# A hybrid attention block: the GLA state scan written in two halves, weights' loads in program order, first scalings without precedence

## The chip, the cores and the metric

The kernel runs on one core of a Trainium2 chip. The metric is the device time of one execution in microseconds (us); the time before is the median of three runs. Engines are named as in the profile: PE multiplies matrices, DVE and POOL work elementwise, ACT evaluates functions and copies, SP only issues DMAs. Each engine works through its own instructions in order; between engines there are semaphores.

## The reference

One encoder block over 1024 tokens of width 1024, in float32. Eight heads of neighbourhood attention (`y_na`) stand beside four heads of bidirectional gated linear attention (GLA); both are projected from the same normalised input, joined, projected out, and followed by a squared-ReLU MLP.

```python
n = rmsnorm(h, ln_g)
proj = n @ w_in                      # q, k, v of both groups, gate r, decay factors z_f, z_b
...
# GLA, per head and direction, in chunks of 64 tokens
A = jnp.where(mask, jnp.einsum('bhnid,bhnjd->bhnij', q_dec, k_inv), 0.0)
o_intra = jnp.einsum('bhnij,bhnje->bhnie', A, v)
contrib = jnp.einsum('bhncd,bhnce->bhnde', k * jnp.exp(b_last - b), v)
def step(S, inp):
    g, c = inp
    return g[..., None] * S + c, S
_, S_prev = lax.scan(step, S0, (decay, contrib))
o = o_intra + jnp.einsum('bhncd,bhnde->bhnce', q_dec, S_prev)
...
h = h + concat(y_na, y_gla) @ w_out
h = h + square(relu(rmsnorm(h) @ w1)) @ w2
```

## The kernel before

Activations lie transposed: features on the 128 partitions, tokens along the free axis, in two halves of 512. Every product of 32-bit precision is made of three matmuls of rounded parts: high by high, low by high, high by low (`product`). A projection block is 128 columns of `w_in`: for each half 8 steps of three 128x512 matmuls.

PE's matmuls are kept in the order of the program (class `Ordered`). All other instructions are ordered by a scheduler that takes what is ready, with precedence for what stands in `tc.high_priority`; a larger offset means further ahead. `tc.keep_in_program_order` takes single instructions out of this freedom. `SOON` is 200, `SOON_W` 100, `SOON_B` 300.

- Start, to about 55 us: x is loaded in four quarters of 256 tokens, scaled and split (`do_x`), and its reciprocal norm `rms` is made (`do_norm`, L220 to L230: ACT Ln, Exp and Square, DVE products). Meanwhile PE makes z (decay factors, banks z0 and z1 of the PSUM tag "mm"), and q and k of head group 0 (banks sb and ob). `z_evac` scales z (zf, L342) and splits it into zT (L343 on ACT, L344 on DVE); `qk_evac` scales q and k for two heads each (qd, kd, L280, and ACT's copies in L281). The tag "mm" has two banks, so projection 4's second half needs z1's.
- `weights` (L164 to L177) brings the weights of one projection block: wf by SP (L169), ACT writes wl = -wf (L173), POOL issues an accumulating DMA that adds the exact weights to it (L174), which leaves the low part, and ACT casts the high part wh (L176). Two buffers of each exist. The first block is split by POOL.
- GLA, heads h = 0 to 3 (`gla_contrib`, `gla_scan`, `gla_within`, `gla_intra`, `gla_inter`): contributions per chunk go to the states st; the scan (L591 forward on the lower partitions, L594 backward on the upper ones) is 28 DVE steps; `gla_within` makes masked scores of half a sequence on PE (a, two banks of tag "s") and DVE copies them under a mask into asb (L586, selF then selB). The second half's scores need the first half's banks. Between these stages PE gets steps of the projections of blocks 8, 5, 9, 1, 3, 6, 7, 11, 10, 12, 16, 20, 13, 17, 21 and so on, as many as the row of `GLA_FILL` for this head says; element i is run at `fill.at(GLA_FILL, h, i)`.
- Neighbourhood attention (about 262 to 450 us), pairs of heads p = 0 to 3: `bias_for` loads the relative bias bt from a DRAM scratch (SP, L742; 16 earlier copies fill the scratch, L443), adds the mask msk (POOL's DMA, L736) on DVE (L747); `softmax` makes scores sc, adds the bias with a running extreme (L802), takes the exponential on ACT (L804) and scales (L806, L807); `turn` transposes (pt). bt0, the first bias tile, lies in memory that head 3's kI occupied.
- Then the output projection and the MLP, which fill the span to its end.

Of the kernel before, what the change touches and what calls it, by code (L numbers as in the profile page):

```python
# [14 lines left out]
ALU = mybir.AluOpType  # L15
# [14 lines left out]
NCH = T // CH  # L30
# [14 lines left out]
)  # L45
FILL_ORDER = (('v', 0), ('r', 0), ('v', 1), ('r', 1), ('q', 1), ('v', 2), ('v', 3), ('r', 3), ('r', 2), ('n', 0), ('k', 0))

# [1 line left out]
SOON = 200  # L49
# [17 lines left out]
def block_kernel(ctx, tc, xT, g_mix, w_in, w_z, rpb, na_mask, gu, gb, g_gla, sel_f, sel_b,  # L67
                 rst, w_out, g_ff, w1, w2, g_fin, out):
    nc = tc.nc
    V, S, DMA, G = nc.vector, nc.scalar, nc.sync, nc.gpsimd  # L70
# [14 lines left out]
    def bank(tag, name):  # L85
        return ps.tile([P, H], F32, tag=tag, name=name)
# [77 lines left out]
    def weights(block, eng=None):  # L164


        with tc.high_priority(offset=SOON_W):
            wf = stg.tile([P, D], F32, tag="wf", name="wf")
            DMA.dma_start(wf, block)  # L169
            if eng is not None:  # L170
                return split(wf, eng)
            wl = stg.tile([P, D], F32R, tag="wl", name="wl")
            tc.keep_in_program_order(S.activation(wl, wf, AF.Copy, scale=-1.0))  # L173
            G.dma_start(wl, block, accum_op=ALU.add)  # L174
            wh = stg.tile([P, D], F32R, tag="wh", name="wh")
            tc.keep_in_program_order(S.copy(wh, wf))  # L176
            return wh, wl  # L177
# [12 lines left out]
    def split(wf, eng=None, steps=1):  # L190
        wh = stg.tile([P, D], F32R, tag="wh", name="wh")
        wl = stg.tile([P, D], F32R, tag="wl", name="wl")
        for i in range(steps):
            c = slice(i * D // steps, (i + 1) * D // steps)
            S.copy(wh[:, c], wf[:, c])
            (eng or V).tensor_tensor(wl[:, c], wf[:, c], wh[:, c].bitcast(F32), op=ALU.subtract)
        return wh, wl
# [70 lines left out]
    def qk_evac(g, which):  # L268

        dic, sc, t = ((qd, 0.125, "q"), (kd, 1.0, "k"))[which]  # L270
        for i in range(2):
            dic[2 * g + i] = (g0 if t == "q" and i else gk).tile([P, T], F32, tag={"k0": "k00", "q0": "k10", "k1": "k20"}.get(f"{t}{i}", "qd1"), name=f"{t}d{2*g+i}")

        def ev(hf, d):
            c = slice(hf * H, (hf + 1) * H)
            for i in range(2):
                dst = dic[2 * g + i]
                a, b = (slice(0, 64), slice(64, 128))[::1 - 2 * i]
                with tc.high_priority(offset=SOON):
                    V.scalar_tensor_tensor(dst[a, c], d[a, :], sc, rms[a, c], op0=ALU.mult, op1=ALU.mult)  # L280
                S.copy(dst[b, c], dst[a, c])  # L281
        return ev
# [152 lines left out]
    def bias_cols(cs):  # L435
        for c in cs:
            for dl in range(3):
                o = 8 * dl + 7 - c
                DMA.dma_start(rpb1[c, :, dl, :, :], rpb[:, :, o:o + CW])
# [6 lines left out]
    with pool("gla", R) as gp:  # L446
# [42 lines left out]
        def make_masks():  # L489
            selF = gp.tile([P, 1, P], F32, tag="selF", name="selF")  # L490
            selB = gp.tile([P, 1, P], F32, tag="selB", name="selB")
            G.dma_start(selF, sel_f)
            G.dma_start(selB, sel_b)
            asb = [gp.tile([P, 4, P], F32, tag=f"asb{i}", name=f"asb{i}") for i in range(2)]
            for a in asb:
                G.memset(a, 0.0)
            masks.extend([selF, selB, asb])
# [23 lines left out]
        def gla_keys(h, b):  # L521

            b3 = b.rearrange("p (n c) -> p n c", c=CH)
            kD = g0.tile([P, T], F32, tag="kD", name=f"kD{h}")
            dec = gp.tile([P, NCH], F32, tag="dec", name=f"dec{h}", bufs=2)
            bl = gp.tile([P, NCH], F32, tag="bl", name=f"bl{h}")
            for (lo, hi, e) in ((0, 64, CH - 1), (64, 128, 0)):
                V.tensor_copy(bl[lo:hi, :], b3[lo:hi, :, e])
            S.activation(dec, bl, AF.Exp, scale=-1.0 / 16)
            V.tensor_tensor(kD.rearrange("p (n c) -> p n c", c=CH), b3,  # L530
                            bl.unsqueeze(2).to_broadcast([P, NCH, CH]), op=ALU.subtract)
            S.activation(kD, kD, AF.Exp, scale=1.0 / 16)
            V.tensor_tensor(kD, kD, kd[h], op=ALU.mult)
            qD = gp.tile([P, T], F32, tag="qD", name=f"qD{h}", bufs=2)
            kI = gp.tile([P, T], F32, tag="kI", name=f"kI{h}", bufs=2)
            S.activation(kI, b, AF.Exp, scale=1.0 / 16)
            V.tensor_tensor(kI, kI, kd[h], op=ALU.mult)
            S.activation(qD, b, AF.Exp, scale=-1.0 / 16)
            V.tensor_tensor(qD, qD, qd[h], op=ALU.mult)
            return dec, kD, qD, kI  # L540

        def gla_ktok(h, kD):

            kt = g0.tile([P, NCH // 2, P], F32, tag="kt", name=f"kt{h}", bufs=2)
            for hf in range(2):
                tb = bank("t", f"kt{h}_{hf}")
                for i in range(4):
                    j = hf * 4 + i
                    PE.transpose(tb[:, i * P:(i + 1) * P], kD[:, j * P:(j + 1) * P], ident)
                S.copy(kt[:, hf * 4:(hf + 1) * 4, :], tb.rearrange("p (a b) -> p a b", a=4))  # L550

            st = gp.tile([P, NCH, P], F32, tag="st", name=f"st{h}")
            G.memset(st[0:64, 0, :], 0.0)
            G.memset(st[64:128, NCH - 1, :], 0.0)
            return kt, st
# [19 lines left out]
        def gla_within(h, hf, qD, kI):  # L575

            selF, selB, asb = masks
            a = [bank("s", f"a{h}_{hf}_{i}") for i in range(2)]
            for i in range(4):
                j = hf * 4 + i  # L580
                for dr_ in range(2):
                    o = 64 * dr_
                    PE.matmul(a[dr_][:, i * P:(i + 1) * P], kI[o:o + 64, j * P:(j + 1) * P],
                              qD[o:o + 64, j * P:(j + 1) * P], start=True, stop=True)
            for sel, src in ((selF, a[0]), (selB, a[1])):
                V.copy_predicated(asb[hf], sel.bitcast(U32).to_broadcast([P, 4, P]),  # L586
                                  src.rearrange("p (a b) -> p a b", a=4))

        def gla_scan(dec, st):
            for i in range(1, NCH - 1):  # L590
                V.scalar_tensor_tensor(st[0:64, i + 1, :], st[0:64, i, :], dec[0:64, i:i + 1],  # L591
                                       st[0:64, i + 1, :], op0=ALU.mult, op1=ALU.add)
                j = NCH - 1 - i
                V.scalar_tensor_tensor(st[64:128, j - 1, :], st[64:128, j, :], dec[64:128, j:j + 1],  # L594
                                       st[64:128, j - 1, :], op0=ALU.mult, op1=ALU.add)
# [48 lines left out]
        for h in range(GH):  # L644
            if not masks:
                make_masks()
            fill.until(("q", h // 2))
            dec, kD, qD, kI = gla_keys(h, bs[h])
            fill.at(GLA_FILL, h, 0)
            kt, st = gla_ktok(h, kD)  # L650
            bias_cols(range(2 * h, 2 * h + 2))
            fill.at(GLA_FILL, h, 1)
            fill.until(("v", h))
            gla_contrib(h, kt, st, 0)
            fill.at(GLA_FILL, h, 2)
            gla_contrib(h, kt, st, 1)
            gla_scan(dec, st)
            fill.at(GLA_FILL, h, 3)
            gla_within(h, 0, qD, kI)
            fill.at(GLA_FILL, h, 4)  # L660
            gla_within(h, 1, qD, kI)
            fill.at(GLA_FILL, h, 5)
            if h + 1 < GH:
                bs[h + 1] = gla_gates(h + 1)
            ob = [gla_intra(h, 0)]
            fill.at(GLA_FILL, h, 6)
            ob.append(gla_intra(h, 1))
            fill.at(GLA_FILL, h, 7)
            sq = [gla_inter(0, ob[0], st, qD)]
            fill.at(GLA_FILL, h, 8)  # L670
            sq.append(gla_inter(1, ob[1], st, qD))
            fill.at(GLA_FILL, h, 9)
            gla_norm(h, 0, ob[0], sq[0])
            fill.at(GLA_FILL, h, 10)
            gla_norm(h, 1, ob[1], sq[1])
# [279 lines left out]
    wf = stg.tile([P, D], F32, tag="wf", name="wf")  # L955
# [337 lines left out]
    with tc.high_priority(offset=150):  # L1293
        for n in range(2):
            p, i = f1.order[n]
# [241 lines left out]
```

## Time and profile before

| | us |
|---|---|
| runs | 1219.82, 1216.45, 1217.22 |
| median | 1217.22 |
| profiled execution | 1217.29 |
| its span, first to last instruction | 1215.5 |
| mean granted clock of PE | 0.986 |

A row of the timeline gives start and length in us, engine, line, operation, output<-inputs, shape and count; in brackets the idle time of the engine just ahead and what ended it. Rows with a count stand for several instructions merged. A row of waits gives engine, operation and line that waited, what it waited for, and then the us in total, the times and the longest. A row of windows is explained where it is used. DMA rows of the chain run from issue to landing.

### The profile page before, as it was taken

To read this page: it belongs to the slowest core of one execution; us is meant where nothing else is said; L and a number is where in the kernel's file an instruction comes from. 1 tells how busy PE (TensorE), PEld (TensorE's weight loads), DVE (VectorE), ACT (ScalarE), POOL (GpSimd) and SP (SyncE) were. 2 spreads that over 40 slices of the span, in tenths; PEclk is the share of its full clock that TensorE was granted. 3 is DMA by queue.
4 is the path that set the end of the run, shared out by engine and by line. 5 is a ranking of instruction groups with operands and counts; after the bars stand their busy time and mean duration, and the time that the engine had idled before them with its cause. 6 is when DMAs were issued, how large, how long until landed. Compare 5 with 4: busy or idle time off the path is not lost.

```text
span 1215.5 us, 15429 instructions
## 1 busy us (share of the span) xinstructions
PE 1158.5 (95%) x5632; PEld 948.7 (78%) x5632; DVE 874.8 (72%) x1558; ACT 665.1 (55%) x1222; POOL 248.3 (20%) x199
## 2 busy tenths in 40 slices
PE   8899899887999999998999999999999999999995
PEld 8778688675877878876778888888888888888775
DVE  8578768735768696675877885876858768587467
ACT  6667566643756674544643744545445454453664
POOL 5100000201120223441103140321403214032004
PEclk9999999998999999999999999999999999999998
DMA  7332231312323324230110111112111111111203
GB/s 233 70 90 56 72 70 36 89 27 80 68 50 83 70 75 164 104 138 1 58 64 18 70 65 56 37 52 70 62 57 38 53 70 57 59 42 52 70 1 139
DMA packets 40283, 84.03 MB, mean 69 GB/s; under 512 B 9264, under 2 KB 20656, under 8 KB 40208
## 3 DMA queue, kind: packets, MB, share of 16 engines
q1 hardware_dynamic: 36608, 71.11, 17.4%
q0 software_dynamic: 3456, 11.94, 5.5%
q8 instruction: 44, 0.72, 0.2%
q14 instruction: 31, 0.25, 0.1%
q10 hardware_dynamic: 144, 0.00, 0.0%
HBM read 78.85 MB, written 5.96 MB: 70 GB/s over the span
## 4 chain that ended last, share of the span: by engine, by line
PE 71%; DVE 15%; ACT 8%; issue 3%; DMA 2%; SPq 0%; POOL 0%; DVEq 0%; ACTq 0%
PE f L114 24%; PE u L114 21%; PE proj L114 13%; PE op L114 5%; PE sc L114 2%; PE o L114 2%; PE no L114 2%; DVE st L594 1%; PE pt L119 1%; DVE st L591 1%; DVE nl L309 1%; DMA bt<-rpb 1%; DVE pl L1010 1%; DVE asb L586 1%; DVE nf L940 1%
## 5 line engine op out<-in xcount | busy, mean ns | idle before, releaser
L1032 ACT CAST ph<-A 128x512 fp32r<-128x512 f32 x166 | 103.0, 621 | 146.5 <-PE f L114 73.6
L1010 POOL TENSOR_TENSOR ul<-uB,uh 128x512 fp32r<-128x512 f32 x84 | 109.1, 1317 | 330.5 <-ACT uh L1045 213.4
L114 PE MATMUL f<-uh,ph 128*128 128x512 f32 x400 | 155.8, 390 | 1.5 <-ACT u L1053 1.4
L114 PE MATMUL proj<-nh,wh 128*128 128x512 f32 x352 | 151.4, 430 | 4.7 <-DVE zf L342 4.7
L114 PE MATMUL f<-ul,ph 128*128 128x512 f32 x400 | 155.8, 389 | 0.1
L114 PE MATMUL f<-uh,pl 128*128 128x512 f32 x400 | 155.7, 389 | 0.0
L1010 DVE TENSOR_TENSOR pl<-A,ph 128x512 fp32r<-128x512 f32 x166 | 112.8, 689 | 52.5 <-ACT ph L1032 52.5
L114 PE MATMUL proj<-nh,wl 128*128 128x512 f32 x352 | 140.0, 398 | 1.5 <-DMA wl<-in_w_in 1.5
L114 PE MATMUL proj<-nl,wh 128*128 128x512 f32 x352 | 139.1, 395 | 0.0
L1192 DVE TENSOR_TENSOR hT<-hT,f 128x512 f32<-128x512 f32 x168 | 113.0, 687 | 19.9 <-PE f L114 19.9
L114 PE MATMUL u<-n,ph 128*128 128x512 f32 x288 | 89.2, 391 | 2.0 <-ACT ph L945 2.0
L114 PEld LDWEIGHTS f<-uh,ph 128*128 128x128 f32 x400 | 75.1, 188 | 17.8 <-ACT u L1053 1.8
L114 PEld LDWEIGHTS f<-ul,ph 128*128 128x128 f32 x400 | 75.1, 188 | 15.9 <-DVE ul L1010 0.4
L114 PEld LDWEIGHTS f<-uh,pl 128*128 128x128 f32 x400 | 75.1, 188 | 15.7
L114 PEld LDWEIGHTS proj<-nh,wh 128*128 128x128 f32 x352 | 67.1, 191 | 23.3 <-issue 10.7
L114 PEld LDWEIGHTS proj<-nh,wl 128*128 128x128 f32 x352 | 66.9, 190 | 17.0 <-DMA wl<-in_w_in 1.9
L1045 ACT CAST uh<-uB 128x512 fp32r<-128x512 f32 x84 | 51.9, 618 | 51.0 <-PE f L114 34.2
L114 PE MATMUL u<-T,ph 128*128 128x512 f32 x256 | 79.2, 391 | 0.1
L114 PE MATMUL op<-y,wh 128*128 128x512 f32 x240 | 77.0, 402 | 0.4 <-DVE y L696 0.4
L114 PEld LDWEIGHTS proj<-nl,wh 128*128 128x128 f32 x352 | 67.4, 191 | 11.9 <-issue 1.7
L804 ACT ACTIVATE xsc<-xsc,sm 128x384 f32<-128x384 f32 (+1 forms) x64 | 37.3, 584 | 59.0 <-DVE sm L802 58.6
L114 PE MATMUL u<-nt,ph 128*128 128x512 f32 x224 | 68.9, 389 | 0.0
(300 smaller groups left out, 2504.5 us busy)
## 6 DMA issues: line engine op xcount, KB each, us to landing
A<-in_w SPq DMA_DIRECT2D x64, 512.0 KB
wf<-in_w_in SPq DMA_DIRECT2D x22, 512.0 KB
wl<-in_w_in POOLq DMA_DIRECT2D x21, 512.0 KB, 6.9
wf<-in_w_out SPq DMA_DIRECT2D x17, 512.0 KB
hT<-in_xT SPq DMA_DIRECT2D x2, 2048.0 KB
xs<-in_xT SPq DMA_DIRECT2D x6, 512.0 KB
out<-hT SPq DMA_DIRECT2D x4, 512.0 KB
out<-hT SPq DMA_DIRECT2D x8, 256.0 KB
```

Source lines behind the costliest of these rows:

```text
L114: m = nc.tensor.matmul(*args, **kw)
L119: tc.keep_in_program_order(nc.tensor.transpose(*args, **kw))
L309: V.scalar_tensor_tensor(nl[:, k, sl], xs[:, k, :], gmix[:, k:k + 1], nh[:, k, sl].bitcast(F32), op0=ALU.mult, op1=ALU.subtract)
L586: V.copy_predicated(asb[hf], sel.bitcast(U32).to_broadcast([P, 4, P]), src.rearrange("p (a b) -> p a b", a=4))
L591: V.scalar_tensor_tensor(st[0:64, i + 1, :], st[0:64, i, :], dec[0:64, i:i + 1], st[0:64, i + 1, :], op0=ALU.mult, op1=ALU.add)
L594: V.scalar_tensor_tensor(st[64:128, j - 1, :], st[64:128, j, :], dec[64:128, j:j + 1], st[64:128, j - 1, :], op0=ALU.mult, op1=ALU.add)
L804: S.activation(x[:, :n], x[:, :n], AF.Exp, scale=-1.0, bias=sm[:, i, 0:1], accum_out=sm[:, i, 1:2])
L940: V.scalar_tensor_tensor(dst, hT[:, d, hf * H:(hf + 1) * H], gff[:, d:d + 1], r, op0=ALU.mult, op1=ALU.mult)
L1010: return kp(eng.tensor_tensor(l, x, h.bitcast(F32), op=ALU.subtract))
L1032: kp(S.copy(ph, x))
L1045: kp(S.copy(uh, x))
L1192: kp(V.tensor_tensor(hT[:, d, c], hT[:, d, c], o[:, s], op=ALU.add))
```

## The change

Four edits. `gla_scan` takes a range of steps; the first half stands where the scan stood, the second behind the first half's masked scores. The last row of `GLA_FILL` gets other numbers. In `weights`, the load on SP and the accumulating DMA on POOL are kept in program order (ACT's two casts were already). And the scalings in `qk_evac` have the offset `SOON * g`, which is 0 for head group 0 and 200, as before, for group 1. No instruction is added or taken away.

```diff
-    (13, 4, 3, 8, 3, 2, 3, 3, 3, 0, 7),
+    (13, 4, 3, 4, 5, 4, 3, 3, 3, 0, 7),
...
-            DMA.dma_start(wf, block)
+            load = DMA.dma_start(wf, block)
             if eng is not None:
                 return split(wf, eng)
+            tc.keep_in_program_order(load)
             wl = stg.tile([P, D], F32R, tag="wl", name="wl")
             tc.keep_in_program_order(S.activation(wl, wf, AF.Copy, scale=-1.0))
-            G.dma_start(wl, block, accum_op=ALU.add)
+            tc.keep_in_program_order(G.dma_start(wl, block, accum_op=ALU.add))
...
-                with tc.high_priority(offset=SOON):
+                with tc.high_priority(offset=SOON * g):
                     V.scalar_tensor_tensor(dst[a, c], d[a, :], sc, rms[a, c], op0=ALU.mult, op1=ALU.mult)
...
-        def gla_scan(dec, st):
-            for i in range(1, NCH - 1):
+        def gla_scan(dec, st, i0, i1):
+            for i in range(i0, i1):
...
             gla_contrib(h, kt, st, 1)
-            gla_scan(dec, st)
+            gla_scan(dec, st, 1, NCH // 2)
             fill.at(GLA_FILL, h, 3)
             gla_within(h, 0, qD, kI)
+            gla_scan(dec, st, NCH // 2, NCH - 1)
             fill.at(GLA_FILL, h, 4)
```

What this does to the order of the instructions shows at three places. Lines of the changed kernel stand one or two further down: L342 is L343 there, L280 is L281, L586 is L587, L591 and L594 are L592 and L595, L742 is L744.

DVE at the start, where the second half of z, q and k of group 0 leaves PSUM; before:

```order
L229 TENSOR_TENSOR nt_516<-nt_516,nu_519 128x256
L230 SCALAR_TENSOR_TENSOR rms_109<-nt_516,rms_109 128x256
L280 SCALAR_TENSOR_TENSOR qd0_157<-sb1_371,rms_109 64x512
L280 SCALAR_TENSOR_TENSOR qd1_158<-sb1_371,rms_109 64x512
L280 SCALAR_TENSOR_TENSOR kd0_159<-ob1_528,rms_109 64x512
L280 SCALAR_TENSOR_TENSOR kd1_160<-ob1_528,rms_109 64x512
L342 TENSOR_TENSOR zf_524<-z1_354,rms_109 64x512
L344 TENSOR_TENSOR zT_116<-zf_524,zT_116 64x512
```

and in the changed kernel:

```order
L230 TENSOR_TENSOR nt_516<-nt_516,nu_519 128x256
L231 SCALAR_TENSOR_TENSOR rms_109<-nt_516,rms_109 128x256
L343 TENSOR_TENSOR zf_524<-z1_354,rms_109 64x512
L281 SCALAR_TENSOR_TENSOR qd0_157<-sb1_371,rms_109 64x512
L281 SCALAR_TENSOR_TENSOR qd1_158<-sb1_371,rms_109 64x512
L345 TENSOR_TENSOR zT_116<-zf_524,zT_116 64x512
L281 SCALAR_TENSOR_TENSOR kd0_159<-ob1_528,rms_109 64x512
L281 SCALAR_TENSOR_TENSOR kd1_160<-ob1_528,rms_109 64x512
```

zf moved ahead of the four scalings, zT between the two pairs; the first half of the tokens (z0) moved in the same way. On ACT, block 8's two casts (L173, L176), which stood between L227 and L221 of the last quarter's norm, now stand behind its L228.

DVE in head 3, from the 17th step of the scan on (the ten L591 at once and the pairs behind them are alike up to there); before:

```order
L594 SCALAR_TENSOR_TENSOR st3_2003<-st3_2003,dec3_1908 64x128
L413 TENSOR_TENSOR qt_2111<-proj12_1_2044,rms_109 128x512
L594 SCALAR_TENSOR_TENSOR st3_2003<-st3_2003,dec3_1908 64x128
L591 SCALAR_TENSOR_TENSOR st3_2003<-st3_2003,dec3_1908 64x128
L594 SCALAR_TENSOR_TENSOR st3_2003<-st3_2003,dec3_1908 64x128 x7
L586 COPY_PREDICATED asb0_715<-selF_711,a3_0_0_2137 128x512
L594 SCALAR_TENSOR_TENSOR st3_2003<-st3_2003,dec3_1908 64x128
L586 COPY_PREDICATED asb0_715<-selB_712,a3_0_1_2138 128x512
L594 SCALAR_TENSOR_TENSOR st3_2003<-st3_2003,dec3_1908 64x128
L586 COPY_PREDICATED asb1_716<-selF_711,a3_1_0_2158 128x512
L586 COPY_PREDICATED asb1_716<-selB_712,a3_1_1_2159 128x512
```

and in the changed kernel (its first row is again the 17th step):

```order
L595 SCALAR_TENSOR_TENSOR st3_2003<-st3_2003,dec3_1908 64x128
L592 SCALAR_TENSOR_TENSOR st3_2003<-st3_2003,dec3_1908 64x128
L595 SCALAR_TENSOR_TENSOR st3_2003<-st3_2003,dec3_1908 64x128 x2
L587 COPY_PREDICATED asb0_715<-selF_711,a3_0_0_2094 128x512
L595 SCALAR_TENSOR_TENSOR st3_2003<-st3_2003,dec3_1908 64x128
L414 TENSOR_TENSOR qt_2123<-proj12_1_2044,rms_109 128x512
L587 COPY_PREDICATED asb0_715<-selB_712,a3_0_1_2095 128x512
L595 SCALAR_TENSOR_TENSOR st3_2003<-st3_2003,dec3_1908 64x128 x7
L587 COPY_PREDICATED asb1_716<-selF_711,a3_1_0_2152 128x512
L587 COPY_PREDICATED asb1_716<-selB_712,a3_1_1_2153 128x512
```

Ahead of asb0's copy under selF stand 20 steps of the scan rather than 26, and qt (the evacuation of projection 12's second half) is behind it. On PE the first half's scores of head 3 moved four fill steps forward, ahead of the last step of projection 12, and five fill steps, not three, follow until the second half's scores. In head 1 asb0's copies moved two scan steps forward, selB past two kd scalings as well; heads 0 and 2 are as before.

SP, where the first bias tile (bt0) is loaded among the weights' loads; wf_2120 and wf_2132 are block 20's load before and in the changed kernel, wf_2320, wf_2446, wf_2650 and wf_2803 those of blocks 13, 17, 21 and 14. Before:

```order
L169 DMA wf_2120<-in_w_in 128x1024
L169 DMA wf_2320<-in_w_in 128x1024
L169 DMA wf_2446<-in_w_in 128x1024
L169 DMA wf_2650<-in_w_in 128x1024
L742 DMA bt0_2309<-rpb2_594 128x2x384
L169 DMA wf_2803<-in_w_in 128x1024
```

and in the changed kernel:

```order
L169 DMA wf_2132<-in_w_in 128x1024
L744 DMA bt0_2309<-rpb2_594 128x2x384
L169 DMA wf_2320<-in_w_in 128x1024
L169 DMA wf_2446<-in_w_in 128x1024
L169 DMA wf_2650<-in_w_in 128x1024
L169 DMA wf_2803<-in_w_in 128x1024
```

bt0 moved ahead of three loads; the next bias tiles moved by one load each, POOL's DMA of msk ahead of one accumulating DMA. At the start of the first softmax (p = 0) DVE now has L802 of the second block of tokens ahead of L806 and L807 of the first. Behind that the two kernels' orders are alike to the end.

## The prediction

> **What bounds the kernel now.** I read the page first, then TensorE's waits grouped by who ended them, then the rows around the three longest, then the granted clock by stretches. PE is the engine to watch (first the page's busy times, then waits: us in total, times, the longest):
>
> ```profile
> PE 1158.5 (95%) x5632; PEld 948.7 (78%) x5632; DVE 874.8 (72%) x1558; ACT 665.1 (55%) x1222; POOL 248.3 (20%) x199
> PE sc L114 <- DVE sm L802: 8.9, 1, 8.9
> PE a L114 <- DVE asb L586: 6.7, 5, 3.7
> PE proj L114 <- DVE zf L342: 4.7, 1, 4.7
> ```
>
> The span of 1215.5 has some 57 us without a matmul. The change touches the code of the three longest waits and leaves PE's work as it is, so I ask only how much of these waits goes, and what the clock does there:
>
> ```profile
> 54.41:57.81 3.40, 3.40 (x9) 2.65 (x8) 1.38 (x2) 0.00 (x0) 2.15 (x5) 0.50 0.30 93
> 242.15:248.98 6.83, 6.38 (x28) 5.28 (x29) 3.42 (x6) 0.08 (x1) 0.00 (x0) 0.50 0.45 88
> 280.64:286.52 5.88, 5.75 (x15) 4.00 (x16) 4.59 (x17) 3.23 (x10) 0.00 (x0) 0.50 0.00 0
> 549.30:552.76 3.46, 1.68 (x7) 1.10 (x7) 3.21 (x3) 0.49 (x1) 3.42 (x2) 1.00 0.02 5
> 552.76:556.18 3.42, 3.42 (x10) 2.63 (x9) 1.74 (x2) 0.63 (x1) 1.95 (x2) 0.50 0.00 0
> ```
>
> The columns are the stretch, its length, busy time of PE, PEld, DVE, ACT, POOL, then the granted clock. Behind each of the three waits stands a stretch at clock 0.50, in which half of PE's busy time is lost: 1.70, 3.19 and 2.88 us. A long wait is thus paid for twice.
>
> **The change, part by part.** *A, the first scalings without precedence.* Before, the fourth quarter's chain runs like this:
>
> ```profile
> 43.87 0.68 DVE L344 TENSOR_TENSOR zT<-zf,zT 64x512 fp32r<-64x512 f32 x1 [1.23 <-ACT zT L343]
> 45.56 0.47 ACT L220 ACTIVATE nt<-ssq,small 128x256 f32<-128x256 f32 x1 [1.41 <-DVE rms L230]
> 46.29 1.06 ACT L173 ACTIVATE wl<-wf 128x1024 fp32r<-128x1024 f32 x1
> 47.24 1.04 ACT L176 CAST wh<-wf 128x1024 fp32r<-128x1024 f32 x1
> 47.66 0.93 POOL L174 DMA_DIRECT2D wl<-in_w_in  x1 [6.18 <-ACT wl L173]
> 48.18 0.51 ACT L221 ACTIVATE rms<-nt,small 128x256 f32<-128x256 f32 x1
> 49.17 0.43 DVE L229 TENSOR_TENSOR nt<-nt,nu 128x256 f32<-128x256 f32 x1 [3.70 <-ACT nt L228]
> 50.16 1.41 DVE L280 SCALAR_TENSOR_TENSOR qd<-sb,rms 64x512 f32<-64x512 f32 x2
> 51.60 1.41 DVE L280 SCALAR_TENSOR_TENSOR kd<-ob,rms 64x512 f32<-64x512 f32 x2
> 53.04 0.68 DVE L342 TENSOR_TENSOR zf<-z,rms 64x512 f32<-64x512 f32 x1
> 53.87 0.47 PE L114 MATMUL proj<-nh,wh 128*128 128x512 f32 x1 [4.71 <-DVE zf L342]
> ...
> 62.21 0.39 PE L114 MATMUL proj<-nl,wh 128*128 128x512 f32 x1
> 62.43 0.39 PE L114 MATMUL proj<-nh,wl 128*128 128x512 f32 x1
> ```
>
> PE has nothing from 49.17 (53.87 less 4.71) until zf has emptied the bank of z1. By the new order three things leave this path. The first zf stands ahead of its scalings, so that ACT's cast of it is done when L344 comes and the 1.23 goes: L220 at 45.56 - 1.23 = 44.33. Block 8's two casts go behind L221 and L228: these begin 1.89 (48.18 less 46.29) sooner again, so L229 starts at 49.17 - 3.12 = 46.05. And the four scalings (53.04 - 50.16 = 2.88) fall behind the second zf, which ends at 53.72 - 6.0 = 47.72. That is 1.45 ahead of PE's 49.17, so the whole 4.71 goes and with it the 1.70 of half clock: **-6.4**. What is late next: the casts now follow L228 at about 46.0, the accumulate of block 8's wl is issued near 47.3, lands (6.9, below) near 54.2, and PE, which first multiplied by it at 62.43 (nh by wl), wants it 6.4 earlier, at 56.0. That cover is 1.8 us; beyond it, each us late costs one.
>
> *H, head 1.* Both copies of asb0 go two scan steps forward (0.38 each, see B), selB also past the two scalings of kd (1.41 us for two in the rows above). The row they relieve:
>
> ```profile
> 141.19 1.13 PE L114 MATMUL a<-qD,kI 64*128 64x128 f32 x14 [1.91 <-DVE asb L586]
> ```
>
> The 1.91 could go entirely, but the copies of asb1 still wait behind the scan, and the bank they free is the next matmul's; I take **-1.0**, between 0 and -1.91.
>
> *B, head 3, scan in halves and the row of the fill table.* Before:
>
> ```profile
> 234.30 0.34 DVE L591 SCALAR_TENSOR_TENSOR st<-st,dec 64x128 f32<-64x128 f32 x1
> 234.68 0.35 DVE L594 SCALAR_TENSOR_TENSOR st<-st,dec 64x128 f32<-64x128 f32 x1
> 235.06 0.69 DVE L413 TENSOR_TENSOR qt<-proj,rms 128x512 f32<-128x512 f32 x1
> 236.48 2.62 POOL L422 TENSOR_TENSOR q<-qt,q 64x512 fp32r<-64x512 f32 x2 [6.29 <-ACT q L418]
> 236.54 4.65 DVE L594 SCALAR_TENSOR_TENSOR st<-st,dec 64x128 f32<-64x128 f32 x7
> 241.22 0.72 DVE L586 COPY_PREDICATED asb<-selF,a 128x512 f32<-128x512 uint32 x1
> 242.00 0.69 PE L114 MATMUL a<-qD,kI 64*128 64x128 f32 x2 [3.70 <-DVE asb L586]
> 243.14 2.07 PE L114 MATMUL a<-qD,kI 64*128 64x128 f32 x14 [0.45 <-DVE asb L586]
> ```
>
> The scan's 28 steps start 0.38 apart where nothing disturbs them (234.30, 234.68); seven beside POOL's two subtractions took 4.65 rather than 2.66. The step at 234.68, ended at 235.03, is the 17th. In the new order 20 steps stand ahead of selF, and qt behind it: the 20th ends at about 236.2, selF at 236.9, then one step, qt (0.69) and selB (0.72) end at 238.8. PE's second half of the scores reached its wait at 238.30 (242.00 less 3.70); now it comes two fill steps sooner (its first half moves 4 steps forward, but 5 steps, not 3, lie between the halves), at 0.69 a step (three 512-column matmuls, 0.22 to 0.23 apart: 62.21, 62.43) near 236.9. selF is just done; two matmuls later selB's bank is missing until 238.8. PE waits some 1.8 where it waited 3.70 + 0.45 = 4.15: -2.3. The 3.19 at half clock loses its cause, but a wait of 1.8 may throttle too. The gain is 2.3 + 3.2 = 5.5 without a throttle, 3.9 with one stretch of 3.4 at half clock (half of PE's time in it, some 1.6). The nearest row is 549.30: 1.78 idle (3.46 less 1.68) were followed by clock 0.50. I take **-3.9**. The collision with POOL moves onto the seven steps behind selB; with its 2.0 the copies of asb1 end near 245.0, and PE, which resumes at 238.9, has 1.1 of scores and 7 fill steps (4.8) and one group of four before it wants them, near 245.1. That is no cover to speak of: 0 to 2 us are at risk.
>
> *C, the neighbourhood bias held ahead of three weights' loads.*
>
> ```profile
> 224.88 0.33 SPq L169 DMA_DIRECT2D wf<-in_w_in  x1
> 268.38 1.04 ACT L173 ACTIVATE wl<-wf 128x1024 fp32r<-128x1024 f32 x1
> 270.39 0.33 SPq L169 DMA_DIRECT2D wf<-in_w_in  x1
> 270.82 0.38 SPq L742 DMA_DIRECT2D bt<-rpb  x1
> 270.82 7.43 DMA bt<-rpb
> 271.01 0.69 DVE L620 TENSOR_TENSOR yg<-ny,o 128x512 f32<-128x512 f32 x1
> 278.34 1.90 DVE L747 SCALAR_TENSOR_TENSOR bt<-bt,msk 128x256 f32<-128x256 f32 x5 [6.65 <-DMA bt<-rpb]
> 280.64 0.69 PE L114 MATMUL sc<-k00p,q 128*128 128x384 f32 x1 [8.94 <-DVE sm L802]
> ```
>
> The bias tile's transfer stood on SP behind the load of block 21 (270.39), which waited for a buffer; DVE then waited 6.65 for it, and PE 8.94 for DVE. It now stands behind the load of block 20 and is released when head 3's last scores have read the memory it takes over, near 240. With 7.43 (say 8 to 10 beside two 512 KB loads) it is there 20 us before it is used. So L747 starts when L620 ends, 271.70, and PE, which came 2.30 after L747 began (280.64 - 278.34), at 274.0: a wait of 2.3 instead of 8.94, -6.6. The 2.88 at half clock goes too. Given back: at full speed PE comes to the transposes of the first block sooner than DVE, which now makes the second block's maxima ahead of the first block's scaling: 1.3 (0 to 2). Net -8.2; with a new half-clock window this idle time hides most of it: **-7.6**.
> Behind bt0 on SP now stand the loads of blocks 13, 17 and 21. Block 13's went at 224.88 and goes at about 240.4; its cast was at 268.38, so 16 us of delay fall into 43 of slack: nothing. The later bias tiles move by one load, with as much slack, and the mask's DMA goes earlier: nothing.
>
> **Sum.** 6.4 + 1.0 + 3.9 + 7.6 = 18.9. The profiled execution took 1217.29 (median of the runs 1217.22, so no correction): **1198.4**. If all these waits and their half clocks vanished, 6.4 + 1.9 + 7.3 + 11.8 = 27.4 would give 1190; with no gain in H and B and 2 us lost there, 1205.
>
> **The rivals.** *The remaining waits don't throttle.* Waits of 1.8 and 2.3 us leave the clock at 1.00; then B is 5.5, C 8.2, the sum 21.1 and the time 1196.2. For it: only waits of 3.7 and more lie ahead of the three half-clock stretches above. Against it: 1.78 us sufficed at 549.30. [...]
>
> *The weights' low halves become the next wait.* An accumulating DMA takes long to land:
>
> ```profile
> wl<-in_w_in POOLq DMA_DIRECT2D x21, 512.0 KB, 6.9
> ```
>
> A gain that pulls PE forward by 6.4 doesn't pull ACT's casts and POOL's issues as far: 1.8 us of cover for block 8. If the casts come 2 to 6 us later than I placed them (behind the copies of qd and kd, say), up to A's gain comes back: 1200 to 1205.
>
> *The bias isn't what holds, or doesn't come early.* If something that the rows don't show releases bt0 only near 270, as it stood before, C gives nothing: 1198.4 + 7.6 = 1206.0. The built order shows the move, so only the release is open.
>
> *Slower: SP is held.* SP issues in order, so a bt0 that is not released holds every load behind it. From bt0's issue at T, PE's scores come T + 7.4 + 2.3 at best, so PE is later than before by T - 271, on before's clock, and block 13's load, cast and accumulate come behind T as well. The gains of A, H and B (11.3) are eaten at T = 282, and past 286 the kernel is slower by 0.3%. Against it: at 270.82 the release had already come.
>
> **How the numbers follow.** The sum as it stands 0.46 (1198.4, give or take 2); no new throttle 0.22 (1196.2); low halves late 0.14 (1200 to 1205); bias not early 0.11 (1206.0); two of the last together, or H and B gone too, 0.04 (1210 to 1215); SP held 0.03 (1221 and more). The range must leave out 2 in 10 at most and take in the bounds of H, B and the give-back in C: 1192 to 1207. A measurement can tell 0.3% (3.6 us) from no change; all but the last two cases are under 1213.6: faster 0.92, same 0.05, slower 0.03.
>
> **What would show it.** A: no PE wait on zf, no half clock near 54, zf ended before 48. B: selF of asb0 in head 3 stands six steps sooner in the scan, a wait near 1.8, mostly on selB. C: the transfer of bt0 right after head 3's last scores, L747 directly behind L620, a PE wait near 2.3. The forecast is wrong if wl's accumulate shows up as a releaser of PE near 50 to 60, if bt0 is still issued beside L747, or if gains here return as longer waits later in the program, where the order is unchanged.

## The result and the profile after

| | us |
|---|---|
| before, median of 4 runs | 1218.06 (1216.45 to 1219.82) |
| changed, median of 4 runs | 1198.32 (1197.52 to 1199.97) |
| ratio | 0.9839, 95% interval 0.9821 to 0.9858 |
| span of the profiled execution | 1196.8, where it was 1215.5 |

The changed kernel is about 19.6 us faster; 1198.4 was predicted, range 1192 to 1207. PE's busy share on the page of the changed kernel:

```profile
PE 1156.5 (97%) x5632; PEld 947.3 (79%) x5632; DVE 873.2 (73%) x1558; ACT 664.8 (56%) x1222; POOL 248.4 (21%) x199
```

and its waits (us in total, times, the longest):

```profile
PE sc L114 <- DVE sm L804: 2.6, 2, 2.2
PE a L114 <- DVE asb L587: 1.8, 2, 1.3
```

The three longest waits of before are gone or cut: zf is missing from the list, asb went from 6.7 to 1.8, sm from 8.9 to 2.6. Of the 1.8 for asb, 1.34 are in head 3; the other 0.42 are in head 2, at 179.73, and stood there before the change as well (0.42 at 187.41). No other wait of PE grew by more than 0.1. To see where the time came from, I put the same matmul's start in both profiles side by side:

| matmul | before | changed | shift | step since the row above |
|---|---|---|---|---|
| head 1, first scores a | 133.36 | 126.80 | -6.56 | A: -6.6 (predicted -6.4) |
| head 1, third la | 144.95 | 137.25 | -7.70 | H: -1.1 (-1.0) |
| first sc | 268.03 | 254.47 | -13.56 | B: -5.9 (-3.9) |
| sc, third group | 287.76 | 268.32 | -19.44 | C: -5.9 (-7.6) |
| span's end | 1215.5 | 1196.8 | -18.7 | +0.7 |

Between the third group of sc and the MLP's last blocks the shift stays within 0.1 of -19.5; one half-clock stretch there only sits elsewhere (552.76 before, 540.84 now). The 0.7 is lost at the last four matmuls, before and now:

```profile
1205.36 1.13 PE L114 MATMUL vf<-fsq,ones 128*128 128x256 f32 x4 [1.74 <-DVE fsq L1440]
1185.80 1.96 PE L114 MATMUL vf<-fsq,ones 128*128 128x256 f32 x4 [1.75 <-DVE fsq L1442]
```

In the changed kernel's profile the clock fell to 0.50 at 1185.96, while they ran; before, it fell at 1208.12, when they were over.

Step A in the changed kernel's timeline:

```profile
44.56 0.47 ACT L221 ACTIVATE nt<-ssq,small 128x256 f32<-128x256 f32 x1 [0.30 <-DVE rms L231]
45.29 0.51 ACT L222 ACTIVATE rms<-nt,small 128x256 f32<-128x256 f32 x1
46.15 1.05 ACT L174 ACTIVATE wl<-wf 128x1024 fp32r<-128x1024 f32 x1
46.27 0.43 DVE L230 TENSOR_TENSOR nt<-nt,nu 128x256 f32<-128x256 f32 x1 [1.81 <-ACT nt L229]
47.27 0.68 DVE L343 TENSOR_TENSOR zf<-z,rms 64x512 f32<-64x512 f32 x1
47.51 0.93 POOL L175 DMA_DIRECT2D wl<-in_w_in  x1 [5.95 <-ACT wl L174]
```

zf ends at 47.95 (47.72 was worked out), the accumulating DMA is issued at 47.51 (47.3). PE finds z1's bank free.

Step H, head 1, whose second half of the scores (last row) no longer waits for asb:

```profile
126.80 0.49 PE L114 MATMUL a<-qD,kI 64*128 64x128 f32 x2 [1.05 <-ACT st L574]
127.90 2.07 PE L114 MATMUL a<-qD,kI 64*128 64x128 f32 x14 [0.61 <-ACT st L574]
133.46 1.16 PE L114 MATMUL a<-qD,kI 64*128 64x128 f32 x16
```

Step B, head 3, and the bias tile's issue on SP:

```profile
228.29 0.74 DVE L587 COPY_PREDICATED asb<-selF,a 128x512 f32<-128x512 uint32 x1
229.09 0.48 PE L114 MATMUL a<-qD,kI 64*128 64x128 f32 x2
230.05 0.71 DVE L587 COPY_PREDICATED asb<-selB,a 128x512 f32<-128x512 uint32 x1
230.80 3.39 DVE L595 SCALAR_TENSOR_TENSOR st<-st,dec 64x128 f32<-64x128 f32 x4
230.87 2.78 POOL L423 TENSOR_TENSOR q<-qt,q 64x512 fp32r<-64x512 f32 x2 [8.60 <-ACT q L419]
230.91 1.13 PE L114 MATMUL a<-qD,kI 64*128 64x128 f32 x14 [1.34 <-DVE asb L587]
232.07 0.38 SPq L744 DMA_DIRECT2D bt<-rpb  x1
```

One copy follows 20 scan steps, the other follows qt, as worked out. PE waits 1.34, all of it for selB's bank: selF's is free at 229.03, when PE comes (229.09), and two matmuls fill 0.48 us until it needs the other. Beside POOL's subtractions the steps behind selB now take longer (four in 3.39 us; ahead of selF, at 226.76 and 227.15, two start 0.39 apart), and nothing waits for that. bt0 leaves 0.03 us after the last scores end (232.04).

Step C, the start of the softmax:

```profile
257.44 0.69 DVE L621 TENSOR_TENSOR yg<-ny,o 128x512 f32<-128x512 f32 x1
258.05 1.89 DVE L749 SCALAR_TENSOR_TENSOR bt<-bt,msk 128x256 f32<-128x256 f32 x5
260.34 0.44 PE L114 MATMUL sc<-k00p,q 128*128 128x384 f32 x1 [2.21 <-DVE sm L804]
```

L749 starts when L621 ends, without a wait for the tile; PE comes 2.29 later (2.30 was taken). But the half clock behind the wait did not go, and a new one stands in head 1. Windows of the changed kernel (stretch, length, busy time of PE, PEld, DVE, ACT, POOL, granted clock):

```profile
127.83:131.24 3.41, 3.34 (x17) 2.92 (x18) 3.15 (x9) 0.02 (x1) 0.00 (x0) 0.50 1.00 269
230.22:240.00 9.78, 9.09 (x57) 7.89 (x58) 8.13 (x13) 5.53 (x8) 4.09 (x4) 1.00 0.65 176
260.94:264.36 3.42, 3.21 (x8) 1.69 (x8) 2.02 (x12) 1.87 (x6) 0.00 (x0) 0.50 0.47 132
264.36:267.77 3.41, 3.41 (x11) 2.75 (x10) 1.45 (x5) 0.79 (x3) 0.00 (x0) 0.50 0.00 0
```

Head 3 stayed at full clock behind its wait; C lost half of 6.62 us of PE, 3.3, more than the 2.88 of before.

### The profile page after: what moved, and what is told of

Same layout as the page of the kernel before. It is cut to its first block, busy times and chain, and to the rows that moved or that the text cites. A ratio compares the mean times of both kernels' runs of the same rounds, so it can differ in the third digit from the quotient of the medians.

```text
span 1196.8 us, 15430 instructions
## 1 busy us (share of the span) xinstructions
PE 1156.5 (97%) x5632; PEld 947.3 (79%) x5632; DVE 873.2 (73%) x1558; ACT 664.8 (56%) x1222; POOL 248.4 (21%) x199
## 4 chain that ended last, share of the span: by engine, by line
PE 76%; DVE 12%; ACT 7%; issue 2%; DMA 1%; POOL 0%; SPq 0%; DVEq 0%; ACTq 0%
PE f L114 24%; PE u L114 21%; PE proj L114 14%; PE op L114 5%; PE sc L114 2%; PE o L114 2%; PE no L114 2%; PE pt L119 1%; PE sb L114 1%; DVE st L595 1%; DVE st L592 1%; PE ob L114 1%; DVE pl L1012 1%; DVE asb L587 1%; DVE nf L942 1%
## 5 line engine op out<-in xcount | busy, mean ns | idle before, releaser
L806 ACT ACTIVATE xsc<-xsc,sm 128x384 f32<-128x384 f32 (+1 forms) x64 | 37.3, 584 | 52.9 <-DVE sm L804 52.6
```

Of the source, the lines that this page charges most:

```text
L806: S.activation(x[:, :n], x[:, :n], AF.Exp, scale=-1.0, bias=sm[:, i, 0:1], accum_out=sm[:, i, 1:2])
```

## The experiments

**The theory**: four independent terms, each a wait of PE and, where it comes, the half clock behind it: A from the scalings, H from the split scan, B from the row of the fill table, C from the order of the loads. **Rivals**: later waits swallow them; or other edits carry them than those named. The kept order of the accumulating DMA, taken back by itself, leaves the order of every engine as it is, so it was not run. First each of the other edits was taken back.

*Scalings with precedence again:*

```diff
-                with tc.high_priority(offset=SOON * g):
+                with tc.high_priority(offset=SOON):
```

> The changed kernel with one edit taken back: the first scalings have the offset 200 for group 0 again. Theory (the terms are separate, each one wait and the half clock behind it): PE waits for zf near 49 again, about 4.7 us, a half-clock stretch follows, and the time is 6.5 us above the changed kernel's 1198.3: 1204.8, ratio to before 0.989. Rival (later waits absorb it, since projections run ahead of the heads): under 3 us, 1201 or less.

Measured: 1204.28, ratio 0.9896 (0.9881 to 0.9911). PE's longest wait:

```profile
PE proj L114 <- DVE zf L343: 4.7, 1, 4.7
```

and two windows of half clock:

```profile
51.28:58.10 6.82, 4.19 (x10) 3.35 (x11) 3.76 (x6) 2.71 (x5) 2.36 (x6) 0.50 0.67 186
239.01:242.42 3.41, 3.41 (x11) 2.52 (x10) 3.23 (x6) 1.63 (x2) 3.15 (x4) 0.50 0.57 172
```

The whole term is back and nothing downstream swallows it. The last row belongs to head 3: its wait, 1.34 as in the changed kernel, here did bring a half clock. (This profile is of the slowest of the four runs, 1206.89.)

*Loads free again:*

```diff
-            tc.keep_in_program_order(load)
```

> The changed kernel with the load of the weights not kept in program order; the accumulating DMA stays kept. Theory: bt0 stands behind block 21's load again and the wait ahead of sc becomes about 9 us; PE loses the 6.7 us of wait, but not a half clock, since that came in both kernels: 5 to 6.5 us, 1204, ratio 0.989. Rival (the accumulating DMA's order did it): within 1 us of 1198.3. Rival (the half clock behind the wait was gained as well, as I predicted): 7.6, 1206.

Measured: 1203.58, ratio 0.9888 (0.9873 to 0.9903). Timeline:

```profile
257.32 0.33 SPq L169 DMA_DIRECT2D wf<-in_w_in  x1
257.75 0.38 SPq L743 DMA_DIRECT2D bt<-rpb  x1
264.71 1.90 DVE L748 SCALAR_TENSOR_TENSOR bt<-bt,msk 128x256 f32<-128x256 f32 x5 [6.08 <-DMA bt<-rpb]
267.01 0.69 PE L114 MATMUL sc<-k00p,q 128*128 128x384 f32 x1 [8.39 <-DVE sm L803]
```

bt0 is behind a weights' load again and the wait with it. The accumulating DMA was still held in order, so it is not what moved the tile.

*Scan in one piece:*

```diff
-            gla_scan(dec, st, 1, NCH // 2)
+            gla_scan(dec, st, 1, NCH - 1)
             fill.at(GLA_FILL, h, 3)
             gla_within(h, 0, qD, kI)
-            gla_scan(dec, st, NCH // 2, NCH - 1)
```

> The changed kernel with the scan in one piece at its old place; the new row of the fill table stays. Theory: only head 1 loses, 2.3 us of waits for asb's bank less what a half-clock stretch there took: 1 to 2.5 us, 1199.3 to 1200.8; head 3 stays within 0.5 us. Rival (the split carries head 3's gain): 5 us or more, 1203.5.

Measured: 1201.57, ratio 0.9867 (0.9852 to 0.9881). That is 0.8 us above the range expected, and the interval overlaps the changed kernel's, so the times alone hardly show this term. In its profile head 1 has the old waits:

```profile
131.76 0.49 PE L114 MATMUL a<-qD,kI 64*128 64x128 f32 x2 [0.22 <-DVE asb L587]
134.16 1.13 PE L114 MATMUL a<-qD,kI 64*128 64x128 f32 x14 [1.92 <-DVE asb L587]
```

Against the changed kernel's first profile, 1.1 us are lost in head 1, although the half clock that stood there is absent here. Another 0.5 goes at a wait for a weights' low half (1.70 at 211.55, where it was 1.21) and 0.6 in head 3, where PE waits 1.87 for asb rather than 1.34. So the split serves head 1 in the main, and head 3 a little.

*The old row of the fill table:*

```diff
-    (13, 4, 3, 4, 5, 4, 3, 3, 3, 0, 7),
+    (13, 4, 3, 8, 3, 2, 3, 3, 3, 0, 7),
```

> The changed kernel with the last row of the fill table as before (8, 3, 2); the scan stays in halves. Theory (the row makes head 3's gain): selF of asb0 stands behind qt and six more scan steps again, PE waits about 4 us for asb's banks in head 3, and a half clock follows: 4 to 5.5 us, 1202.3 to 1203.8. Rival (the split makes it): within 1 us of 1198.3.

Measured: 1203.24, ratio 0.9881 (0.9864 to 0.9897). DVE and PE in head 3:

```profile
228.77 4.65 DVE L595 SCALAR_TENSOR_TENSOR st<-st,dec 64x128 f32<-64x128 f32 x7
233.45 0.72 DVE L587 COPY_PREDICATED asb<-selF,a 128x512 f32<-128x512 uint32 x1
...
234.23 0.48 PE L114 MATMUL a<-qD,kI 64*128 64x128 f32 x2 [3.70 <-DVE asb L587]
235.37 1.01 PE L114 MATMUL a<-qD,kI 64*128 64x128 f32 x6 [0.65 <-DVE asb L587]
```

With the scan still in halves, the 3.70 is back to the hundredth, for the same reason: seven steps beside POOL's two subtractions (228.71 to 231.33) ahead of selF. So B is the table row's, but for the 0.5 of wait that the split takes off.

Then the changed kernel once more, to see what of its profile is chance.

> The changed kernel once more. If half-clock stretches are set by where free-running windows happen to fall, the profile shows the same waits of PE to 0.3 us, but the stretch behind head 1's waits (127.8 to 131.2 in the first profile) may be gone or another one added, each worth about 1.7 us; the time is 1198.3, give or take 2. If the waits alone decide, the stretches are the same ones at the same places.

Measured: 1198.07, ratio 0.9844 (0.9829 to 0.9858). PE's waits that the change touches agree with the first profile's to 0.1 us. Two others do not: one for vf late in the MLP is 1.3 shorter, one at the start (for nh, ACT) 0.8 longer. Some of its windows:

```profile
127.88:131.30 3.42, 3.42 (x19) 2.81 (x16) 3.16 (x9) 0.00 (x0) 0.00 (x0) 0.50 1.00 273
261.00:264.41 3.41, 3.41 (x11) 1.94 (x11) 2.23 (x11) 1.93 (x7) 0.00 (x0) 0.50 0.32 94
264.41:267.82 3.41, 3.41 (x16) 2.54 (x16) 2.24 (x5) 0.47 (x2) 0.00 (x0) 1.00 0.02 5
530.65:534.06 3.41, 3.41 (x8) 2.72 (x9) 2.60 (x3) 0.63 (x1) 2.81 (x2) 0.50 0.00 0
```

Head 1's stretch came again, C's lasted one window of 3.41 instead of two, and two more came, at 530.65 and at 1168.94: the waits are mostly the kernel's, the stretches partly the execution's.

Four undone terms against this run's ratio, times 1217: 6.3, 5.4, 2.8 and 4.5, together 19.0; the whole change by the same ratio 19.0. Each difference has an uncertainty of about 2.5 us by the intervals, so that the two sums agree to the tenth is chance; but nothing big is shared between the edits.

*The loads' order alone*, on the kernel before:

> The kernel before with the loads and the accumulating DMA kept in program order, nothing else. Theory (terms are separate): the wait ahead of sc falls from 8.9 to about 2.6, a half-clock stretch stays: 5 to 6.5 us faster, 1211.5, ratio 0.995. Rival (bt0's wait for head 3's scores holds block 13's load up to a wait of PE): gain under 3 us and a wait on wl or wh near 285.

Measured: 1210.59, ratio 0.9944 (0.993 to 0.9957), 6.8 us, just above the 5 to 6.5 expected. Timeline:

```profile
244.76 0.38 SPq L743 DMA_DIRECT2D bt<-rpb  x1
245.23 24.77 SPq L169 DMA_DIRECT2D wf<-in_w_in  x3
...
273.19 0.44 PE L114 MATMUL sc<-k00p,q 128*128 128x384 f32 x1 [2.22 <-DVE sm L803]
274.00 0.45 PE L114 MATMUL sc<-k10p,q 128*128 128x384 f32 x1 [0.37 <-DVE sm L803]
```

The held loads start only behind bt0, and PE has no new wait for weights. A tile released so late that the loads would be missed was not tried.

*What is left of C.* If the remaining 2.6 us are DVE's order, another engine can prepare the first tile while DVE is busy:

```diff
+            if p == 0:
+                G.tensor_scalar(bt[:, :, 0:3, :], bt[:, :, 0:3, :], 8.0, None, op0=ALU.mult)
+                for i in range(2):
+                    for o, src, m in ((3, 1, rows), (5, 0, rows), (0, 0, msk[:, 0:3, :])):
+                        n = 3 if o == 0 else 2
+                        G.tensor_tensor(bt[:, i, o:o + n, :], bt[:, i, src:src + n, :], m, op=ALU.add)
+                return bt
...
+                if p == 0 and b == 0:
+                    tc.keep_in_program_order(ex)
```

(ex is the exponential of L806.)

> The changed kernel, but POOL makes the first pair's bias tile (times 8, then the masks added: 7 instructions) as soon as its transfer and the mask's have landed, in place of DVE's six at L749, and the first two exponentials stay behind block 13's casts on ACT. The result is the same. Theory (what is left of the wait ahead of sc is DVE's order, 2.3 from L749's start to PE): the wait goes from 2.6 in two parts to under 1.0 and the half-clock stretch of two windows behind it goes too; 1.8 + 3.3 less up to 1.3 for the transposes: 3.5 to 5, that is 1193.3 to 1194.8, ratio 0.980. Rival (the stretch comes anyhow, from the softmax's start): 1.5 to 2, 1196.5. [...]

Measured: 1193.63, ratio 0.9803 (0.979 to 0.9816): 5.0 us faster than the changed kernel by the ratios of one session, 4.4 by the medians, and the fastest of all. POOL and PE in its timeline:

```profile
235.75 2.14 POOL L747 TENSOR_SCALAR bt<-bt 128x768 f32<-128x768 f32 x1 [0.60 <-DMA bt<-rpb]
243.30 5.61 POOL L751 TENSOR_TENSOR bt<-bt,msk 128x256 f32<-128x256 f32 x6 [5.41 <-DMA msk<-in_na_mask]
258.61 0.44 PE L114 MATMUL sc<-k00p,q 128*128 128x384 f32 x1 [0.41 <-DVE sm L811]
261.55 0.41 PE L119 MATMUL pt<-ident,xsc 128*128 128x128 f32 x2 [0.90 <-DVE sm L817]
```

and the window behind the wait:

```profile
260.00:268.00 8.00, 7.05 (x36) 5.14 (x34) 6.32 (x23) 4.20 (x11) 0.00 (x0) 1.00 0.36 94
```

The tile is ready at 248.9, nine us early; the wait shrinks to 0.41, the transposes wait 0.90, and the clock stays at 1.00. So the half clock behind C was that wait's, and not the softmax's. Not all of the gain is C's, though. From the first sc to the third group this profile gains 4.1 us on the changed kernel's first profile and 2.6 on its second, where C's half clock lasted one window. The rest comes near 530 to 545, where this execution had no half clock and the changed kernel's had one stretch or two; whether the edit does that or chance is open.

*The same with the first exponential free*, without the last two lines of the diff:

> As bias_pool, but the scheduler puts the first exponential ahead of block 13's two casts on ACT. Theory (low halves of weights have little cover once PE comes earlier): the cast waits for the first softmax, some 4 us later; cast, accumulating DMA and its 6.9 us end about 267.5, PE wants them near 265: a wait of 1 to 3 us on wl, so 1 to 3 us above bias_pool. Rival (cover is ample): same as bias_pool within 1 us.

Measured: 1196.79, ratio 0.9828 (0.9804 to 0.9852), about 3 above bias_pool, but the four runs lie between 1192.74 and 1200.08 and the intervals overlap. ACT and PE of the profiled run (1199.09):

```profile
260.42 1.04 ACT L174 ACTIVATE wl<-wf 128x1024 fp32r<-128x1024 f32 x1
...
263.63 0.41 PE L119 MATMUL pt<-ident,xsc 128*128 128x128 f32 x2 [1.43 <-ACT xsc L813]
...
269.04 0.50 PE L114 MATMUL proj<-nh,wl 128*128 128x512 f32 x1 [1.55 <-DMA wl<-in_w_in]
```

Block 13's cast, at 254.81 in the changed kernel, waits until 260.42, and PE waits 1.55 for the low half, until 269.04. From the first sc to the fourth group, behind this wait, 2.2 us are lost against bias_pool's profile. The two profiles differ by 6.8 at the end. Their mean granted clocks are 0.989 here and 0.994 there, which over the 1197.3 us of this span is up to some 6 us (an estimate from these figures), so much of the rest can be clock. The wait is the rival "low halves become the next wait": it is there once a cast comes 5.6 us late, and the change itself did not reach it.

## Why the prediction was right, and where its terms were not

- **A** held in every part: the 1.23 ahead of L344 went, the casts moved, zf ended 0.2 from where it was put, no half clock followed (1.00 from 47.27 to 54.00), block 8's low half came in time. 6.6 against 6.4; the run that takes it back lost 6.3 us.
- **H** was right in size (1.1 against 1.0) by luck. The waits of head 1 for asb went entirely, 1.91 and 0.23, and a half-clock stretch at 127.83, which the prediction did not have, took 1.5 back (14 scores in 2.07 us rather than 1.16, three matmuls of the projection in 1.40 rather than 0.81). It stands behind two waits for ACT's copies (1.05 and 0.61) that the kernel had before the change too (1.06 and 0.61). It came in the changed kernel's two profiles, with the old row of the fill table (matmuls of the projection 0.63 long from 129.45, where 0.39 is usual) and with the bias on POOL (128.95 to 132.37). Behind the same two waits, of 1.04 to 1.06 and 0.61 to 0.62, it did not come before the change, nor with the scalings' precedence, the loads free or the scan in one piece.
- **B**: the order came as worked out, but the wait is 1.34, not 1.8: the sum left out that two matmuls of scores (0.48) stand between selF's bank and selB's. The term that was mis-sized most is "a wait of 1.8 may throttle too", for which I took 1.6 off: in the changed kernel's first profile the clock stayed at 1.00 behind it (230.22 to 240.00). So 2.8 of wait and the 3.2 at half clock went, and 5.9 were gained. It was no sure thing either way: with the scalings' precedence again, half clock followed the same wait of 1.34 (239.01 to 242.42). The row it was judged by was no surer: its wait, 1.78 in the stretch from 549.30, stands in all ten profiles (1.8 in each list of waits); half clock followed it before (552.76) and in the changed kernel's second profile (530.65), but in the first the clock stayed at 1.00 behind it (1.79 until 532.40; no half clock before 540.84, behind another wait).
- **C**: the wait went as forecast, 8.94 to 2.6 (2.3 and 0.37, which I left out). The term that was mis-sized is the half clock: I had the 2.88 as gone, or mostly hidden behind the transposes (0.6 net) if it came again. With the wait of 2.2 kept it came again: as two windows in the changed kernel's first profile (worth 3.3) and with the scan in one piece (262.76 to 269.58), as one in its second profile, and with the loads' order alone (a matmul of the projection took 0.63 at 275.32, where those at 270 took 0.39). So 5.9 in the first profile and 5.4 to 6.8 by the timed runs, not 7.6. That the wait itself brings it is shown by the run in which POOL makes the bias tile: with the wait it came in these four profiles, and with 0.41 in its place the clock stayed at 1.00 (260 to 268).
- The sum was right because B was 2.0 too small and C 1.7 too large, both mostly by the clock. The distance of 0.1 from the median is luck of that size.
- **The rivals.** "The remaining waits don't throttle" was true of head 3's in the changed kernel's first profile and false of C's. Nor did half clock follow single long waits alone: in the 3.42 us ahead of head 1's stretch (124.41 to 127.83), with waits of 1.05 and 0.61, PE was busy 1.83, and half clock followed. A bias that doesn't come early, or a held SP, did not happen: bt0 left at 232.07 and the loads behind it at 232.54, with slack to spare. Nor did the weights' low halves become the next wait: PE waits for no wl between 50 and 60.

## What to carry to other kernels

Here a wait of the bounding engine was worth its length plus the half clock behind it (zf: 4.71 and 1.70), and the second part was gained for sure only where little of the wait remained (0.41 ahead of sc, where 2.2 kept a stretch of 3.41 or 6.83 us; 1.34 in head 3 went either way): count what the engine will still wait, not only what goes. SP issued in order (bt0 at 257.75 behind a weights' load at 257.32, the held loads from 245.23 behind bt0 at 244.76), so a small transfer that is needed on the path belongs ahead of large ones that have slack. A step that only has to be done before a deadline (here adding bias and mask, ready at 248.9 for a use at 258.61) can be put on an engine that is idle long before it. What then becomes ready earlier must not pass work with a nearer deadline on a third engine, as the exponential passed block 13's casts on ACT (260.42 rather than 254.81).

## What was not expected of the hardware

The same kernel with the same waits at its heads and softmax had half-clock stretches at different places in two executions: two windows or one behind C, none or one at 530 us and at 1169 us. Each window costs about 1.7 us, half of 3.41 (in the stretch at 540.84 matmuls of 512 columns started 0.43 us apart, at full clock 0.23). Five runs of that kernel spread over 3.9 us (1196.85 to 1200.78), but the clock does not explain this by itself: the slowest and the median one both had a mean granted clock of 0.990.

In the profiles of before and of the changed kernel (the first), all changes of the clock lie on one grid of 3.41 us, to 0.01 us, so each window of this grid can be set against the clock of the next. A row below is a window at full clock from 20 us on in which PE was busy less than 2.1 us:

| profile, window's start | PE busy | clock of the next |
|---|---|---|
| before, 272.87 | 0.00 | 0.50 |
| before, 238.74 | 0.15 | 0.50 |
| before, 51.00 | 0.55 | 0.50 |
| changed, 257.53 (C's wait) | 1.04 | 0.50 |
| before, 1204.71 | 1.13 | 0.50 |
| changed, 537.43 | 1.32 | 0.50 |
| before, 47.59 | 1.58 | 1.00 |
| changed, 530.60 | 1.62 | 1.00 |
| before, 549.35 | 1.63 | 0.50 |
| changed, 1165.48 | 1.64 | 1.00 |
| changed, 1182.55 | 1.66 | 0.50 |
| changed, 124.41 (head 1) | 1.83 | 0.50 |
| before, 139.75 | 1.97 | 1.00 |
| before, 214.84 | 2.03 | 1.00 |
| before, 614.20 | 2.05 | 1.00 |

Behind windows with 2.15 us and more no half clock came in these two profiles. Head 3's wait in the changed kernel fell across a border of the grid (230.23): 2.69 and 2.73 us of PE were left in the two windows, and the clock stayed. Counted from the span's start the two grids lie half a period apart (54.41 and 127.83 are 21.5 periods), so the same wait can fall differently on them. That this alone makes the choice is not shown: 1.62 and 1.63 us busy, around the same wait, were followed by different clocks. Nor do the rows settle the way back: of the windows at half clock, one with 3.34 us busy was released (127.83), one with 3.21 was followed by another (260.94), and so was the first of the two with 6.74 together with the scan in one piece (262.76), which had 3.33 or more. What decides there stays open.
